# The opening of a one-layer encoder kernel: GpSimd's sums cut and held, square sums on ScalarE, PSUM banks laid out by name

## The chip, the cores and the metric

The kernel runs on one core of a Trainium2 chip. A core has TensorE (PE in the profile; its weight loads are PEld), VectorE (DVE), ScalarE (ACT), GpSimd (POOL) and SyncE (SP), which issues most transfers. The metric is the device time of one execution in microseconds; the median of several runs is compared.

## What is computed

One layer of a macaron encoder over 1024 frames of width 1024 in float32: half a SwiGLU feed-forward (inner width 2816), stick-breaking attention with 16 heads, and half a second SwiGLU feed-forward, each behind an RMS norm.

```python
def rms_norm(x, gain):
    xf = x.astype(jnp.float32)
    y = xf * lax.rsqrt(jnp.mean(xf * xf, axis=-1, keepdims=True) + NORM_EPS)
    return (y * gain.astype(jnp.float32)).astype(x.dtype)

def swiglu(xn, w_in, w_out):
    gate, up = jnp.split(xn @ w_in, 2, axis=-1)
    return (jax.nn.silu(gate) * up) @ w_out
...
        x = x + 0.5 * swiglu(rms_norm(x, n1), wi1, wo1)
        x = x + stick_breaking_attention(rms_norm(x, mix_norm), *mix_params)
        x = x + 0.5 * swiglu(rms_norm(x, n2), wi2, wo2)
```

(The last three lines stand in a loop of one layer.) The change touches the norm in front of the first feed-forward, the first feed-forward itself, and the step from its first half to its second.

## The kernel before

**Numbers.** Every float32 operand of a product is split into two parts of the type that TensorE multiplies: `hi`, a rounded copy, and `lo`, the difference. A product is then three matmuls (hi hi, hi lo, lo hi; lines 308 to 310 in `mm3`, line 324 in `mm3_late`, which puts the third of each behind by four so that a late `lo` doesn't stop it). The copy is mostly ScalarE's, the difference GpSimd's or VectorE's (`split`, lines 196 and 197).

**Opening (lines 669 to 849).** The 1024 rows of x lie in eight blocks of 128, loaded in the order 4, 5, 6, 7, 0, 1, 2, 3. For each block: the sum of squares in two halves (`square`: ScalarE's or VectorE's, with an accumulator), the mean of the halves (`rate`, line 707, on GpSimd) and its power of -1/2 (line 711, GpSimd), the scaling of the rows (`scale`, line 714, VectorE), 128x128 transposes on TensorE into the banks `kb` (`turn_x`, line 743), and out of the banks `xh` on ScalarE (`high_x`, line 751) and `xl` on VectorE (`low_x`, line 754). Meanwhile the weights of the first pair of column blocks are split (`high`, `low`). The products of `first_pair` (line 849) follow in four steps: three units on rows 4 and 5 (256 columns), three units on rows 6 and 7, the fourth unit on all four, and all four units on rows 0 to 3. The callbacks `second_half` and `first_rows` put the transposes of the next rows ahead of the second, third and fourth step. Before the first transposes TensorE multiplies zeros (`IDLE`, line 687).

Rows 0 to 3 and 4 to 7 are also combined for the method of the later rounds, which needs seven products of half-size blocks in place of eight. `whole_x` (line 766, GpSimd) forms xh + xl of rows 4 to 7 in two halves of the width (`d` = 0 into `tl[0]`, `d` = 1 into `tl[3]`); `first_rows` subtracts these and others (lines 754 and 846).

**Order.** `go` chains the opening's instructions on each engine by hand: each may be issued only after the one that `go` put there last (`tc.issue_after`, an edge of order on one engine, not a wait between engines). The rest is ordered by the framework from priorities and its own estimate of times. `marks["open"]` puts the weight work of round 1 behind the opening.

**Rounds (`ffn_in`).** Ten rounds q = 1 to 10 follow; each makes the gate and the up projection of two column blocks by `seven`: products into banks `ka`, `kc` and two of `kb`, a copy out of a bank by ScalarE (line 498), a sum out of a bank by VectorE (line 502). `prepare` makes the seven weight operands, with sums on VectorE (line 475) and `unit`s, among them `s3`. Silu is ScalarE's (line 545), the product with the gate GpSimd's (line 552).

**Banks.** PSUM has eight banks of 128x512. `bank` takes a tile by name from the pool of the stage; a name gets its place when it is first asked for. In the opening that order is kc0, kb0, kb1, kb2, kb3, ka0, ka1, kc1. The next stage (`ffn_out`) lays out its own names ahead by `lay_banks`: ma0, ma1, mb0, mb1, ma2, ma3, mb2, mb3. Its first products go into ma0 to ma3 in turn; a bank may be written once the old one at its place has been read.

Of the kernel before, what the change touches and what calls it, by code (L numbers as in the profile page):

```python
# [67 lines left out]

IDLE = 13

# [43 lines left out]
def macaron_kernel(ctx, tc, x, g1, w1_in, w1_out, gm, w_qkv, gq, gk, w_o, g2, w2_in, w2_out, out):  # L114
# [51 lines left out]

    def lay_banks():

        p, _ = psum[-1]
        for tag, i in (("ma", 0), ("ma", 1), ("mb", 0), ("mb", 1), ("ma", 2), ("ma", 3), ("mb", 2), ("mb", 3)):  # L170
            p.tile([P, NHALF], F32, name=f"{tag}{i}", bufs=1)

# [123 lines left out]
    def go(engine, emit):  # L296

        with following(marks.get(engine)):
            marks[engine] = emit().ins
# [130 lines left out]
    def ffn_in(pl, w_in, keep, tl, hb, right, last):  # L430
# [35 lines left out]
        def prepare(raw, behind=None):  # L466
# [59 lines left out]
        for q in range(1, NQ):  # L526
# [17 lines left out]
            for g in gs.values():  # L544
                act.activation(g, g, AF.Silu)

# [117 lines left out]
    with pools(*RAWS) as pr:  # L664
# [3 lines left out]
        with banks("ps1"), pools(*STREAM) as pa:  # L668
            with pools("x") as px, pools("xs", side="right") as pl:
# [34 lines left out]
                def rate(tb, n=1):  # L704
                    to = slice(tb, tb + n)
                    for i in range(tb, tb + n):
                        go("pool", lambda: pool_e.tensor_scalar(
                            mean[:, i : i + 1], ss[:, 2 * i : 2 * i + 1], ss[:, 2 * i + 1 : 2 * i + 2], EPS,
                            op0=ALU.add, op1=ALU.add,
                        ))  # L710
                    go("pool", lambda: pool_e.tensor_tensor(r[:, to], mean[:, to], power.to_broadcast([P, n]), op=ALU.pow))

                def scale(tb, h):
                    go("dve", lambda: dve.tensor_scalar(
                        xs[tb][:, HALVES[h]], rows_of[tb][:, HALVES[h]], r[:, tb : tb + 1], None, op0=ALU.mult
                    ))

# [11 lines left out]
                def low(j, part, d, engine="pool", behind=None):  # L729
                    (hi, lo), src = us[j, part][d], src_of[j, part, d]  # L730
                    if behind is not None:
                        go("pool", lambda: pool_e.tensor_tensor(lo[:, 0, 0:1], behind, behind, op=ALU.mult))
                    e = pool_e if engine == "pool" else dve
                    go(engine, lambda: e.tensor_tensor(lo, src, hi.bitcast(F32), op=ALU.subtract))
# [27 lines left out]

                def whole_x(tbs):
                    c, q = slice(tbs[0] * P, (tbs[-1] + 1) * P), slice(tbs[0] % 4 * P, (tbs[-1] % 4 + 1) * P)
                    for d, t in ((0, tl[0]), (1, tl[3])):
                        go("pool", lambda: pool_e.tensor_tensor(
                            t[:, :, q], xh[:, 4 * d : 4 * d + 4, c].bitcast(F32),
                            xl[:, 4 * d : 4 * d + 4, c].bitcast(F32), op=ALU.add,
                        ))
# [14 lines left out]
                behind = xs[5][:, D - 1 :]  # L784
                for d in range(2):
                    high(0, 0, d)
                high(1, 0, 0, "dve")
                tps = turn_x((4, 5), range(KD))
                for d in range(2):
                    low(0, 0, d, behind=None if d else behind)  # L790
                high_x(tps, (4, 5))
                low_x(tps, (4, 5))
                high(1, 0, 1)
                for d in range(2):
                    low(1, 0, d)
                for tb in (6, 7):
# [9 lines left out]
                behind = xs[7][:, D - 1 :]  # L806
                for d in range(2):
                    high(1, 1, d)
                for d in range(2):
                    low(1, 1, d, behind=None if d else behind)  # L810
# [542 lines left out]
```

## Time and profile before

| | |
|---|---|
| median of 3 runs | 1954.4 us (1949.22 to 1956.27) |
| profiled execution, its own time | 1954.04 us |
| its span | 1952.3 us |
| mean granted clock of TensorE | 0.995 |
| busy share: TensorE, VectorE, ScalarE, GpSimd | 98%, 64%, 50%, 58% |
| moved by DMA | 259.70 MB, 133 GB/s mean |

The span goes from the first to the last instruction of the program. A row of the timeline has the start in us from the span's start, the busy time, the engine, the line of the kernel, the operation, out<-in by the kernel's names without buffer numbers, the shapes, the count of instructions that it merges, and in brackets the idle time of the engine before it and what ended it. A row by tile has the count and the shortest, median and longest duration in ns. A row by stretches has the stretch, its length, the busy time with the count of PE, PEld, DVE, ACT and POOL, the granted clock (1.00 is full speed), the DMA share and GB/s. The chain of work is followed back from the last instruction: at each step to what released it. A wait for several semaphores is put down to the one that came last.

### The profile page before, as it was taken

The numbers are of one execution on the slowest core, as the hardware profiler recorded it, in microseconds if no ns is written. First come the engines' busy times: TensorE is split into PE (matmuls) and PEld (weight loads), VectorE is DVE, ScalarE is ACT, GpSimd is POOL, SyncE is SP. The second block draws the span as 40 slices with busy tenths as digits, with TensorE's granted clock in tenths as the row PEclk, the third lists the DMA queues.
The fourth block names the chain that finished last, engine by engine and source line by source line (L and its number), as shares of the span: only waits on it lengthen the run. The fifth ranks groups of instructions, "written<-read, shape, count | busy, mean of one in ns | idle before, by whom it ended". The sixth has DMA issues, their size and how long they took to land.

```text
span 1952.3 us, 26654 instructions
## 1 busy us (share of the span) xinstructions
PE 1910.8 (98%) x9357; PEld 1626.4 (83%) x9357; DVE 1249.9 (64%) x1727; ACT 977.8 (50%) x1787; POOL 1122.7 (58%) x997
## 2 busy tenths in 40 slices
PE   7999999999999999999999999999999999999999
PEld 7778888887888899898889887788888888888887
DVE  7855555545665757878877788467645645547645
ACT  5433333343334457777777787344433443343332
POOL 6766666765545746556556564214666666755554
PEclk8999999999999999999999999999999999999999
DMA  5233332337997410111011135421323332369973
GB/s 200 68 100 119 103 103 87 124 106 254 324 329 256 166 34 28 38 44 55 28 39 44 50 116 170 158 78 54 129 92 113 109 103 87 124 205 345 330 269 144
DMA packets 169560, 259.70 MB, mean 133 GB/s; under 512 B 11729, under 2 KB 82385, under 8 KB 169425
## 3 DMA queue, kind: packets, MB, share of 16 engines
q1 hardware_dynamic: 169280, 258.00, 38.9%
q8 instruction: 73, 1.20, 0.3%
q14 instruction: 63, 0.51, 0.1%
q10 hardware_dynamic: 144, 0.00, 0.0%
HBM read 197.66 MB, written 60.29 MB: 132 GB/s over the span
## 4 chain that ended last, share of the span: by engine, by line
PE 84%; DVE 7%; POOL 3%; ACT 3%; issue 2%; DMA 1%; DVEq 0%; SPq 0%; ACTq 0%; POOLq 0%
PE ka L308 6%; PE ka L309 6%; PE ka L310 6%; PE kc L310 4%; PE kc L308 4%; PE kc L309 4%; PE ma L308 4%; PE ma L309 4%; PE ma L310 4%; PE bq L308 4%; PE bq L309 4%; PE bq L310 4%; PE kb L310 3%; PE kb L308 3%; PE kb L309 3%; PE bo L1099 3%
## 5 line engine op out<-in xcount | busy, mean ns | idle before, releaser
L197 POOL TENSOR_TENSOR rp<-raw,rp 128x1024 fp32r<-128x1024 f32 x84 | 210.8, 2514 | 175.4 <-ACT rp L196 156.0
L197 POOL TENSOR_TENSOR u<-sf,u 128x512 fp32r<-128x512 f32 x160 | 227.7, 1426 | 133.2 <-ACT u L196 130.7
L197 POOL TENSOR_TENSOR u<-raw,u 128x512 fp32r<-128x512 f32 x128 | 183.8, 1438 | 159.5 <-ACT u L196 158.8
L1059 POOL TENSOR_TENSOR w<-w,om 128x512 f32<-128x512 f32 (+4 forms) x128 | 140.8, 1104 | 115.0 <-DVE om L1052 88.7
L196 ACT ACTIVATE u<-sf 128x512 fp32r<-128x512 f32 x160 | 100.5, 630 | 199.1 <-PE kb L309 86.3
L446 DVE TENSOR_TENSOR h<-h 128x512 f32<-128x512 f32 x110 | 135.4, 1234 | 85.5 <-POOL h L552 84.8
L196 ACT ACTIVATE rp<-rh 128x1024 fp32r<-128x1024 f32 (+1 forms) x78 | 76.5, 984 | 207.3 <-issue 67.3
L308 PE MATMUL bq<-wqh,xh 128*128 128x384 f32 x512 | 174.6, 341 | 0.0
L310 PE MATMUL bq<-wqh,xl 128*128 128x384 f32 x512 | 172.2, 336 | 0.0
L309 PE MATMUL bq<-wql,xh 128*128 128x384 f32 x512 | 172.1, 336 | 0.0
L574 DVE TENSOR_TENSOR raw<-raw 128x1024 f32<-128x1024 f32 (+1 forms) x60 | 87.4, 1459 | 113.2 <-DMA raw<-w_out 96.9
L196 ACT ACTIVATE u<-raw 128x512 fp32r<-128x512 f32 x128 | 80.3, 631 | 150.6 <-PE ka L309 100.8
L308 PE MATMUL ka<-xh,u 128*128 128x512 f32 x352 | 138.0, 392 | 3.5 <-ACT s L498 3.5
L308 PE MATMUL ma<-rp 128*128 128x512 f32 x352 | 137.8, 392 | 2.7 <-DVE h L502 2.7
L309 PE MATMUL ka<-xl,u 128*128 128x512 f32 x352 | 137.6, 391 | 0.0
L310 PE MATMUL ka<-xh,u 128*128 128x512 f32 x352 | 137.5, 391 | 0.0
L310 PE MATMUL ma<-rp 128*128 128x512 f32 x352 | 137.4, 390 | 0.0
L309 PE MATMUL ma<-rp 128*128 128x512 f32 x352 | 137.4, 390 | 0.0
L1050 ACT ACTIVATE w<-bz,f 128x512 f32<-128x512 f32 (+2 forms) x192 | 112.4, 585 | 44.6 <-PE bz L1046 39.4
L552 POOL TENSOR_TENSOR h<-h,g 128x512 f32<-128x512 f32 x80 | 112.9, 1411 | 36.1 <-DVE h L502 33.1
L475 DVE TENSOR_TENSOR sf<-raw 128x512 f32<-128x512 f32 x80 | 81.3, 1017 | 78.0 <-POOL u L197 78.0
L197 DVE TENSOR_TENSOR rp<-rh,rp 128x1024 fp32r<-128x1024 f32 (+1 forms) x70 | 113.2, 1635 | 22.1 <-ACT rp L196 19.6
(308 smaller groups left out, 5520.4 us busy)
## 6 DMA issues: line engine op xcount, KB each, us to landing
raw<-w_out SPq DMA_DIRECT2D x120, 512.0 KB, 5.6
raw<-w_in SPq DMA_DIRECT2D x86, 512.0 KB, 3.6
k<-h SPq DMA_DIRECT2D x154, 256.0 KB, 2.1
rh<-k SPq DMA_DIRECT2D x64, 512.0 KB, 6.2
raw_qkv<-w_qkv SPq DMA_DIRECT2D x64, 192.0 KB, 3.0
x_keep<-x SPq DMA_DIRECT2D x32, 256.0 KB, 3.5
x<-x_keep SPq DMA_DIRECT2D x32, 256.0 KB, 5.2
raw<-w_out SPq DMA_DIRECT2D x24, 256.0 KB, 4.2
```

The lines of the kernel that those rows point to most:

```text
L196: first = act.activation(hi, raw, AF.Copy).ins
L197: return first, (engine or dve).tensor_tensor(lo, raw, hi.bitcast(F32), op=ALU.subtract).ins
L308: pe.matmul(dst, ah, bh, start=start and i == 0, stop=False, skip_group_check=onto)
L309: pe.matmul(dst, ah, bl, start=False, stop=False, skip_group_check=onto)
L310: pe.matmul(dst, al, bh, start=False, stop=stop and i == n - 1, skip_group_check=onto)
L446: dve.tensor_tensor(src, hb[of[0]], hb[of[1]], op=getattr(ALU, of[2]))
L475: dve.tensor_tensor(f[n], x, y, op=op)
L552: pool_e.tensor_tensor(h, h, gs[k], op=ALU.mult)
L574: dve.tensor_tensor(w[0], w[0], w[1], op=getattr(ALU, W_OF[m][2]))
L1050: act.activation(to, z, AF.Sigmoid, scale=state["f", half][:, sign, tb % 4, hd : hd + 1])
L1059: pool_e.tensor_tensor(wt[:, c1 : c0 + n], wt[:, c1 : c0 + n], om[:, c1 - 1 : c0 + n - 1], op=ALU.mult)
L1099: pe.matmul(ot[:, :n], vv, t[:, c : c + n], start=start, stop=stop)
```

## The change

- 18 products of zeros ahead of the first transposes instead of 13.
- The opening lays out its banks by name: kc0, ka0, ka1, kb0, kb1, kb2, kb3, kc1.
- The means go from GpSimd (one small operation for each block) to VectorE (one for each call of `rate`); the power stays on GpSimd.
- All square sums of rows 0 to 3 are ScalarE's (three halves were VectorE's).
- Row block 4 is scaled by ScalarE; the copy of one first weight half goes from ScalarE to VectorE.
- `whole_x` takes one half of the width at a time, in two pieces of 128x512 instead of one of 128x1024. Only rows 4 and 5, half 0, stay ahead of the scalings of rows 0 to 3. The rest follows them: the first of these is held by a one-column GpSimd operation that reads row block 3's scaled rows.
- Rows 0 and 1 are scaled before the means of rows 2 and 3 are formed.
- In round 2 the four Silus may be issued on ScalarE only after the copy for `s3`, as `prepare` has last made it.

```diff
-IDLE = 13
+IDLE = 18
...
-    def lay_banks():
+    def lay_banks(names=("ma0", "ma1", "mb0", "mb1", "ma2", "ma3", "mb2", "mb3")):
...
-        split(src, hi, lo, engine)
+        marks["unit"], _ = split(src, hi, lo, engine)
...
             us["s3"] = unit(pl, f["s3"], pool_e)
+            marks["s3"] = marks["unit"]
...
-                act.activation(g, g, AF.Silu)
+                with following(marks["s3"] if q == 2 else None):
+                    act.activation(g, g, AF.Silu)
...
+                lay_banks(("kc0", "ka0", "ka1", "kb0", "kb1", "kb2", "kb3", "kc1"))
                 idle = bank("kc")
...
-                    for i in range(tb, tb + n):
-                        go("pool", lambda: pool_e.tensor_scalar(
-                            mean[:, i : i + 1], ss[:, 2 * i : 2 * i + 1], ss[:, 2 * i + 1 : 2 * i + 2], EPS,
-                            op0=ALU.add, op1=ALU.add,
-                        ))
+                    parts = ss[:, 2 * tb : 2 * (tb + n)].rearrange("p (t h) -> p t h", h=2)
+                    go("dve", lambda: dve.scalar_tensor_tensor(
+                        out=mean[:, to], in0=parts[:, :, 0], scalar=EPS, in1=parts[:, :, 1], op0=ALU.add, op1=ALU.add,
+                    ))
...
+                    if engine == "act":
+                        go("act", lambda: act.activation(to, x_, AF.Copy, scale=by))
+                    else:
+                        go("dve", lambda: dve.tensor_scalar(to, x_, by, None, op0=ALU.mult))
+
+                def hold(to, tb):
+                    last = xs[tb][:, D - 1 :]
+                    go("pool", lambda: pool_e.tensor_tensor(to, last, last, op=ALU.mult))
...
-                def whole_x(tbs):
+                def whole_x(tbs, d, behind=None):
...
+                    if behind is not None:
+                        hold(t[:, 0, q.start : q.start + 1], behind)
+                    for k in (0, 2):
+                        ks = slice(4 * d + k, 4 * d + k + 2)
                         go("pool", lambda: pool_e.tensor_tensor(
-                            t[:, :, q], xh[:, 4 * d : 4 * d + 4, c].bitcast(F32),
-                            xl[:, 4 * d : 4 * d + 4, c].bitcast(F32), op=ALU.add,
+                            t[:, k : k + 2, q], xh[:, ks, c].bitcast(F32), xl[:, ks, c].bitcast(F32), op=ALU.add
                         ))
...
-                for tb in (4, 5):
+                for tb, engine in ((4, "act"), (5, "dve")):
                     for h in range(2):
-                        scale(tb, h)
+                        scale(tb, h, engine)
...
-                square(0, 0)
-                square(0, 1)
-                square(1, 0)
-                square(1, 1, "dve")
+                for tb in range(2):
+                    for h in range(2):
+                        square(tb, h)
                 rate(0, 2)
-                whole_x((4, 5))
+                whole_x((4, 5), 0)
...
                     for tb in (2, 3):
-                        square(tb, 0)
-                        square(tb, 1, "dve")
-                    rate(2, 2)
-                    whole_x((6, 7))
-                    for tb in range(4):
+                        for h in range(2):
+                            square(tb, h)
+                    for tb in (0, 1):
                         for h in range(2):
                             scale(tb, h)
+                    rate(2, 2)
+                    for tb in (2, 3):
+                        for h in range(2):
+                            scale(tb, h)
+                    whole_x((6, 7), 0, behind=3)
+                    whole_x((4, 5), 1)
+                    whole_x((6, 7), 1)
```

More of the change, by code (lines that the diff above doesn't have):

```diff
@@ L165, in bank @@
         return p.tile([P, NHALF], F32, name=f"{tag}{i}", bufs=1)
-    def lay_banks():
+    def lay_banks(names=("ma0", "ma1", "mb0", "mb1", "ma2", "ma3", "mb2", "mb3")):
         p, _ = psum[-1]
-        for tag, i in (("ma", 0), ("ma", 1), ("mb", 0), ("mb", 1), ("ma", 2), ("ma", 3), ("mb", 2), ("mb", 3)):
-            p.tile([P, NHALF], F32, name=f"{tag}{i}", bufs=1)
+        for name in names:
+            p.tile([P, NHALF], F32, name=name, bufs=1)
     def any_bank(tags=ROUND):
@@ L705, in rate, with scale @@
                     to = slice(tb, tb + n)
-                    for i in range(tb, tb + n):
-                        go("pool", lambda: pool_e.tensor_scalar(
-                            mean[:, i : i + 1], ss[:, 2 * i : 2 * i + 1], ss[:, 2 * i + 1 : 2 * i + 2], EPS,
-                            op0=ALU.add, op1=ALU.add,
-                        ))
[L711 to L716, printed above, removed]
+                    parts = ss[:, 2 * tb : 2 * (tb + n)].rearrange("p (t h) -> p t h", h=2)
+                    go("dve", lambda: dve.scalar_tensor_tensor(
+                        out=mean[:, to], in0=parts[:, :, 0], scalar=EPS, in1=parts[:, :, 1], op0=ALU.add, op1=ALU.add,
+                    ))
+                    go("pool", lambda: pool_e.tensor_tensor(r[:, to], mean[:, to], power.to_broadcast([P, n]), op=ALU.pow))
+                def scale(tb, h, engine="dve"):
+                    to, x_, by = xs[tb][:, HALVES[h]], rows_of[tb][:, HALVES[h]], r[:, tb : tb + 1]
+                    if engine == "act":
[5 more added lines that the diff above has]
+                    go("pool", lambda: pool_e.tensor_tensor(to, last, last, op=ALU.mult))
                 us, src_of = {}, {}
@@ L731, in low @@
                     if behind is not None:
-                        go("pool", lambda: pool_e.tensor_tensor(lo[:, 0, 0:1], behind, behind, op=ALU.mult))
+                        hold(lo[:, 0, 0:1], behind)
                     e = pool_e if engine == "pool" else dve
@@ L761, in low_x @@
                         less(xl[:, k, c], tp, k, xh[:, k, c].bitcast(F32))
-                def whole_x(tbs):
+                def whole_x(tbs, d, behind=None):
                     c, q = slice(tbs[0] * P, (tbs[-1] + 1) * P), slice(tbs[0] % 4 * P, (tbs[-1] % 4 + 1) * P)
-                    for d, t in ((0, tl[0]), (1, tl[3])):
+                    t = tl[3 * d]
+                    if behind is not None:
+                        hold(t[:, 0, q.start : q.start + 1], behind)
+                    for k in (0, 2):
+                        ks = slice(4 * d + k, 4 * d + k + 2)
                         go("pool", lambda: pool_e.tensor_tensor(
-                            t[:, :, q], xh[:, 4 * d : 4 * d + 4, c].bitcast(F32),
-                            xl[:, 4 * d : 4 * d + 4, c].bitcast(F32), op=ALU.add,
+                            t[:, k : k + 2, q], xh[:, ks, c].bitcast(F32), xl[:, ks, c].bitcast(F32), op=ALU.add
                         ))
@@ L780, in macaron_kernel @@
                     rate(tb)
-                for tb in (4, 5):
+                for tb, engine in ((4, "act"), (5, "dve")):
                     for h in range(2):
-                        scale(tb, h)
-                behind = xs[5][:, D - 1 :]
-                for d in range(2):
-                    high(0, 0, d)
+                        scale(tb, h, engine)
+                high(0, 0, 0)
+                high(0, 0, 1, "dve")
                 high(1, 0, 0, "dve")
                 tps = turn_x((4, 5), range(KD))
-                for d in range(2):
-                    low(0, 0, d, behind=None if d else behind)
+                low(0, 0, 0, behind=5)
+                low(0, 0, 1)
                 high_x(tps, (4, 5))
@@ L793, in macaron_kernel @@
                 high(1, 0, 1)
-                for d in range(2):
-                    low(1, 0, d)
+                low(1, 0, 0)
+                low(1, 0, 1)
                 for tb in (6, 7):
@@ L805, in macaron_kernel @@
                         scale(6 + d, h)
-                behind = xs[7][:, D - 1 :]
                 for d in range(2):
                     high(1, 1, d)
-                for d in range(2):
-                    low(1, 1, d, behind=None if d else behind)
-                square(0, 0)
-                square(0, 1)
-                square(1, 0)
-                square(1, 1, "dve")
+                    low(1, 1, d, behind=None if d else 7)
+                for tb in range(2):
+                    for h in range(2):
+                        square(tb, h)
                 rate(0, 2)
-                whole_x((4, 5))
+                whole_x((4, 5), 0)
                 def second_half():
```

## The prediction

> **What bounds the kernel now.** The page first: TensorE is busy for 98% of the span, so only time in which it stands still, or runs at a low granted clock, can be won.
>
> ```profile
> span 1952.3 us, 26654 instructions
> PE 1910.8 (98%) x9357; PEld 1626.4 (83%) x9357; DVE 1249.9 (64%) x1727; ACT 977.8 (50%) x1787; POOL 1122.7 (58%) x997
> ```
>
> Then the view of who waited for whom: the total wait in us, how often, the longest. Three of its rows are TensorE's over the whole span, the last is ScalarE's in the first 90 us.
>
> ```profile
> PE kb L743 <- DVE xs L714: 8.3, 4, 3.6
> PE ka L308 <- ACT s L498: 3.5, 3, 2.4
> PE ma L308 <- DVE h L502: 2.7, 1, 2.7
> ...
> ACT xh L751 <- PE kb L743: 17.3, 7, 9.9
> ```
>
> The first is the opening: the transposes (L743) wait for VectorE's scaled rows (L714). The second lies in the first feed-forward, the third where that stage hands its PSUM banks to the next. The fourth says that ScalarE has room in the opening. The view by stretches gives the granted clock, the figure behind the five busy times:
>
> ```profile
> 5.24:8.66 3.42, 1.64 (x7) 0.89 (x5) 2.06 (x7) 2.18 (x6) 2.09 (x4) 1.00 1.16 315
> 8.66:12.07 3.41, 3.26 (x16) 3.26 (x16) 2.27 (x7) 2.29 (x6) 2.76 (x3) 0.50 1.01 380
> 12.07:15.49 3.42, 3.42 (x30) 3.42 (x30) 3.42 (x8) 3.42 (x10) 2.60 (x3) 1.00 1.09 376
> ...
> 35.96:39.38 3.42, 0.11 (x1) 0.11 (x2) 3.42 (x3) 0.00 (x0) 2.97 (x2) 0.50 0.00 0
> 39.38:42.79 3.41, 3.41 (x15) 3.31 (x16) 0.83 (x2) 2.50 (x4) 0.00 (x0) 0.50 0.23 82
> ...
> 462.63:466.04 3.41, 3.11 (x7) 2.48 (x8) 2.24 (x4) 1.06 (x1) 2.19 (x1) 0.50 0.82 281
> ```
>
> The reader is to see that a stretch of 3.41 us in which TensorE worked 1.64 us or less is followed by one at half clock. So a stall costs its own length and then up to 1.7 us more. Last, the chain of work, with start and length of each piece, shows the opening's path:
>
> ```profile
> 6.93 0.67 POOL mean L707
> ...
> 7.67 0.57 POOL r L711
> ...
> 8.27 0.50 DVE xs L714
> ...
> 8.81 3.43 PE kb L743 x15
> 12.24 5.75 PE ka L324 x48
> ...
> 20.87 1.76 PE kb L743 x16
> ...
> 42.31 5.76 PE kc L324 x24
> ```
>
> **Why VectorE is late at 32 us.** The timeline of VectorE, and of GpSimd beside it (start, busy time, operation, count, idle time before it):
>
> ```profile
> 25.36 2.76 DVE L699 SCALAR_TENSOR_TENSOR xs<-x 128x512 f32<-128x512 f32 x1
> ...
> 30.87 1.70 DVE L714 TENSOR_SCALAR xs<-x,r 128x512 f32<-128x512 f32 x4
> 32.78 6.83 DVE L714 TENSOR_SCALAR xs<-x,r 128x512 f32<-128x512 f32 x4 [0.22 <-POOL r L711]
> ...
> 31.97 0.77 POOL L711 TENSOR_TENSOR r<-mean,power 128x2 f32<-128x2 f32 x1
> 32.72 4.82 POOL L766 TENSOR_TENSOR tl<-xh,xl 128x1024 f32<-128x1024 f32 x2
> ...
> 54.31 1.30 POOL L846 TENSOR_TENSOR tl<-tl,tl 128x512 f32<-128x512 f32 x1 [15.38 <-DVE tl L754]
> ```
>
> Four scalings take 1.70 us where GpSimd runs no sum (30.87) and 6.83 beside its two sums of 128x1024 (32.78). A square takes 2.76 beside such a sum; alone 0.69 (the median below). One engine holds the other off for a whole instruction.
>
> **The change, step by step.** It moves no transfer, and no queue of DMAs.
>
> *Start: means on VectorE, 18 zero products, row 4 scaled on ScalarE.* The mean for row 5, 0.67 us on the path, becomes one 128x1 operation of VectorE with two columns in, which the trace doesn't have. It costs nothing at least, and at most about the 0.67 that it replaces; the nearest row, of the same engine and width, has 0.15, which I take:
>
> ```profile
> 72.51 0.15 DVE L474 TENSOR_SCALAR sf<-h 128x1 f32<-128x1 f32 x1
> ...
> 10.62 3.40 DVE L754 SCALAR_TENSOR_TENSOR xl<-kb,g_sb,xh 128x256 fp32r<-128x256 f32 x8 [1.14 <-ACT xh L751]
> ...
> L695 ACT ACTIVATE xs<-x x6: 617/624/632, 6.1 to 18.1; 128x512 f32<-128x512 f32 x6
> ...
> L699 DVE SCALAR_TENSOR_TENSOR xs<-x x3: 683/693/1618, 6.1 to 15.5; 128x512 f32<-128x512 f32 x3
> ```
>
> So row 5 is scaled from about 7.75 and its transposes start near 8.3, not at 8.81. The five added zero products, at full clock and 0.23 us from start to start (from 458.71 and 459.85 below, five steps), run into the wait for row 5 and end near 7.7: they delay nothing. TensorE then works some 2.9 us of 5.24:8.66, and the half clock behind it should go. All 16 transposes then take 1.76 (20.87) in place of 3.43 for 15, and end near 10.1 instead of 12.24: 2.1 us at most. But VectorE's eight corrections (3.40 us, now from about 9.7) end at 13.1, and the first 24 products wait for them; they end near 13.6, against 12.24 + 5.75 / 2 = 15.12. I take **1.5**, between 0 (landing rows or GpSimd's differences set the pace instead) and 2.1. Row 4's two scalings (2 x 0.62) lie on ScalarE before the first bank is full, and one raw copy leaves it for VectorE in exchange.
>
> *Square sums of rows 0 to 3 on ScalarE.* Three halves move, 3 x 0.62 = 1.9 us, and VectorE loses its two slowed squares (5.6 us from 25.36 to the scalings at 30.87). ScalarE's room covers them: its reads of the banks start near 19.9 (20.87 less 1.5, and a bank filled), take about 3.4 like the corrections, then four squares 2.5: near 25.8. Without that cover rows 2 and 3 are late one for one. The mean of rows 0 and 1 now stands in VectorE's order ahead of the eight corrections and waits for ScalarE's squares; by its count of six operations of 0.62 behind row 7's these end near 19.4, before the corrections can start, so 0.
>
> *GpSimd's sums in pieces, held.* Only (4,5), half 0, stays ahead of the scalings: two pieces of 128x512, 1.30 each by the row at 54.31. VectorE ends the corrections that stood before 25.36 near 23.9, may wait for a piece until 24.9, scales rows 0 and 1 (1.70) to 26.6, forms two means, GpSimd takes the powers (0.77), at 27.6 to 28.1, and rows 2 and 3 are scaled by 29.8. TensorE asks for them at 31.95 - 1.5 = 30.45. The wait goes:
>
> ```profile
> 31.95 0.60 PE L743 MATMUL kb<-ident,xs 128*128 128x128 f32 x2
> 35.39 0.33 PE L743 MATMUL kb<-ident,xs 128*128 128x128 f32 x1 [2.83 <-DVE xs L714]
> 39.27 3.04 PE L743 MATMUL kb<-ident,xs 128*128 128x128 f32 x13 [3.56 <-DVE xs L714]
> ```
>
> Idle 2.83 + 3.56 = **6.4**. The 13 transposes need 13 x 0.11 = 1.4 instead of 3.04, and 0.5 us of products ran at half clock to 42.79: **1.85** together. The hold waits for the last scaling; behind it on GpSimd stand six pieces (7.8 us), from 30 to 38, in time that is idle today (15.38 before 54.31). VectorE reads PSUM then, and needs the first two pieces near 36; they end near 32.5. Behind them stands a weight difference whose product TensorE reaches only at about 60. Late next: the scalings again; the margin at 30.45 is 0.7 to 1.5 us, thin.
>
> *Banks by name.* Today the next stage's third bank is the one that the last product of the stage before fills:
>
> ```profile
> 458.71 0.39 PE L308 MATMUL ma<-rp 128*128 128x512 f32 x1
> ...
> 459.85 0.39 PE L310 MATMUL ma<-rp 128*128 128x512 f32 x1
> 462.93 0.79 PE L308 MATMUL ma<-rp 128*128 128x512 f32 x1 [2.69 <-DVE h L502]
> ...
> 462.19 0.68 DVE L502 TENSOR_TENSOR h<-kb,s 128x512 f32<-128x512 f32 x1
> 462.79 1.22 DVE L197 TENSOR_TENSOR rp<-raw,rp 128x1024 fp32r<-128x1024 f32 x1
> ```
>
> TensorE issues six products into two banks, then waits for L502 to read kb3. By first use the order is kc0, kb0 to kb3, ka0, ka1, kc1, and the next stage's first four are places 0, 1, 4, 5: place 4 is kb3. In the new order these are kc0, ka0, kb1, kb2, all read earlier. The 2.69 goes, and of the half-clock stretch 3.1 / 2 = 1.55: **4.2**. Late next is the third chunk's operand, ready at 464.0 (L197) and asked for at 458.71 + 48 x 0.23 = 469.7: nothing.
>
> *Silu after the copy of s3, second round.* The stall of 2.4 in that round:
>
> ```profile
> 125.64 0.63 ACT L545 ACTIVATE g<-g 128x512 f32<-128x512 f32 x1 [5.67 <-DVE g L502]
> ...
> 127.33 0.50 PE L308 MATMUL ka<-xh,u 128*128 128x512 f32 x1 [2.36 <-ACT s L498]
> ```
>
> ScalarE's read of the bank stands behind a Silu that waits for VectorE. The mark, though, is the s3 of the gate itself, copied before its products began; as the order stands I cost the edge at **0**. With another order it may gain 2.4 + 1.7 = 4.1, or lose as much if a late copy holds four Silus.
>
> Sum: 1.5 + 6.4 + 1.85 + 4.2 = 13.95. The profiled execution took 1954.04 (1.74 around its span), 0.4 below the median of 1954.4. 1954.04 - 13.95 = **1940**.
>
> [...] 15 transposes filled 8.66:12.07, and the next stretch was granted 1.00. [...]
>
> **Rivals.**
> - *The stall at 127 us goes too*: 1936. For: a Silu stands in the way there. Against: the mark is another copy. 0.15.
> - *Opening alone*; the bank handover meets another late operand: 1954.0 - 9.75 = 1944. For: the operands come from the same three busy engines. Against: 5.7 us of margin. 0.15.
> - *Half the opening*: rows 2 and 3 are 2 to 4 us late; with the half clock behind, 4 to 6 lost: 1944 to 1946, and 1950 if the banks fail too. For: the thin margin. 0.18.
> - *No change*: the engines behind TensorE give it back, 1952 to 1956. For: their chain runs without slack into the first products after the opening. Against: it starts earlier by as much. 0.05.
> - *Slower*: the held sums starve. One sum waited out 9.30 us of VectorE's back-to-back operations on SBUF:
>
> ```profile
> L846 POOL TENSOR_TENSOR tl<-tl,tl x4: 1276/1297/9299, 54.3 to 67.3; 128x512 f32<-128x512 f32 x4
> ```
>
> If that met two of the six, 2 x 8 = 16 and two half clocks make 19 lost: 1959. It decides from 14 us lost. Against: beside VectorE's PSUM reads a sum took its 1.30. 0.05. [...]
>
> **How the numbers follow.** The forecast as written has 0.42. A change within 0.5%, 9.8 us, can't be told from none, so faster means below 1944.6: 0.42 + 0.15 + half of 0.15 = 0.65; same 0.30 (the rest of that, the half opening, no change); slower 0.05. The range leaves a tenth at each end: 1934 (both stalls gone, 2 us better), 1952 above. The likeliest case's own range is 1937 to 1943.
>
> **What would show it.** Right: no wait of L743 for L714 after 20 us, clock 1.00 from 5 to 50 us, products behind the first rows' transposes from 32 to 33 instead of 42.31, no wait of ma for L502. Wrong: rows 2 and 3 scaled after 31 us, a new wait in the first seven products, or the handover at its old length.

## The result and the profile after

The changed kernel takes 1935.53 us (median of four runs, 1933.84 to 1936.71) against 1952.52 for the kernel before beside it (1949.22 to 1956.27): a ratio of 0.9912, 95% interval 0.989 to 0.9933, so 17.0 us less. The forecast was 1940.0. The profiled execution shows 20.2 less (a span of 1932.1 against 1952.3). Both numbers are explained below, and why they differ.

First the page and TensorE's rows in the view of who waited for whom (us in all, times, longest). The rows of kb and ma are gone, and that of ka is at 1.9 instead of 3.5.

```profile
span 1932.1 us, 26665 instructions
PE 1905.4 (99%) x9362; PEld 1622.9 (84%) x9362; DVE 1243.5 (64%) x1726; ACT 981.8 (51%) x1794; POOL 1115.5 (58%) x994
...
PE ka L308 <- ACT s L499: 1.9, 2, 1.5
```

Then the opening in the timeline of TensorE, VectorE and GpSimd. Transposes are now L751, scalings L720, means L710, corrections L762, sums L778, the hold L724.

```profile
30.45 1.91 PE L751 MATMUL kb<-ident,xs 128*128 128x128 f32 x16
32.12 0.71 PE L324 MATMUL kc<-xh,u 128*128 128x512 f32 x2
...
37.67 2.59 PE L751 MATMUL kb<-ident,xs 128*128 128x128 f32 x16
40.02 0.70 PE L324 MATMUL ka<-xh,u 128*128 128x512 f32 x2
...
23.85 1.82 DVE L720 TENSOR_SCALAR xs<-x,r 128x512 f32<-128x512 f32 x4
25.59 0.15 DVE L710 SCALAR_TENSOR_TENSOR mean<-ss 128x2 f32<-128x2 f32 x1
26.56 1.67 DVE L720 TENSOR_SCALAR xs<-x,r 128x512 f32<-128x512 f32 x4 [0.82 <-POOL r L713]
...
34.13 2.73 DVE L762 SCALAR_TENSOR_TENSOR xl<-kb,g_sb,xh 128x512 fp32r<-128x512 f32 x4 [2.71 <-ACT tl L849]
36.77 2.71 DVE L762 SCALAR_TENSOR_TENSOR tl<-kb,g_sb,tl 128x512 f32<-128x512 f32 x4
...
21.65 2.55 POOL L778 TENSOR_TENSOR tl<-xh,xl 128x512 f32<-128x512 f32 x2
28.32 0.20 POOL L724 TENSOR_TENSOR tl<-xs 128x1 f32<-128x1 f32 x1 [1.79 <-DVE xs L720]
28.59 7.52 POOL L778 TENSOR_TENSOR tl<-xh,xl 128x512 f32<-128x512 f32 x6
```

The scalings of rows 2 and 3 take 1.67 instead of 6.83 and end at 28.2; the 16 transposes run through from 30.45 in 1.91, and the products follow at 32.12 instead of 41.96. Six pieces of GpSimd's sums lie behind the hold.

The same program was profiled a second time, and so was the kernel before. The table has the start of some of TensorE's pieces in each, from the timelines.

| piece of TensorE | before | changed | | before, again | changed, again | |
|---|---|---|---|---|---|---|
| first product of the opening | 11.93 | 9.62 | -2.31 | 10.54 | 10.04 | -0.50 |
| transposes of rows 0 to 3 | 31.95 | 30.45 | -1.50 | 31.37 | 30.87 | -0.50 |
| products behind them | 41.96 | 32.12 | -9.84 | 41.83 | 32.54 | -9.29 |
| products behind the next 16 transposes | 49.57 | 40.02 | -9.55 | 50.36 | 40.44 | -9.92 |
| sixth product of the first seven | 86.60 | 76.08 | -10.52 | 87.40 | 76.51 | -10.89 |
| round 2, behind the stall that stood at 127 | 131.78 | 118.77 | -13.01 | 131.01 | 119.22 | -11.79 |
| end of the rounds (first ma) | 458.71 | 445.17 | -13.54 | 457.93 | 445.62 | -12.31 |
| behind the handover (first mb) | 493.05 | 475.09 | -17.96 | 490.84 | 475.54 | -15.30 |
| attention, the piece ahead of the wait at 926 | 924.33 | 907.05 | -17.28 | 922.28 | 906.87 | -15.41 |
| behind that wait (bz) | 926.33 | 907.88 | -18.45 | 924.68 | 909.31 | -15.37 |
| behind the wait at 994 (bz) | 994.08 | 973.85 | -20.23 | 992.76 | 975.57 | -17.19 |
| last stage | 1918.38 | 1897.88 | -20.50 | 1917.33 | 1899.77 | -17.56 |

The right-hand pair agrees with the medians. The left-hand pair has more besides: half clocks of the kernel before at 8.66, 128 and 462 us, which its second profile lacks, and a wait in attention that the first profile of the changed kernel happened to miss. The second profile of the kernel before has half clocks of its own: 10.24 us of them from 34.38, where the first has 6.83, and 3.41 from 925.26, behind the first wait in attention.

### The profile page after: what moved, and what is told of

The parts are those of the page before. It is cut to its first block, busy times and chain, and to the rows that moved or that the text cites. A ratio compares the mean times of both kernels' runs of the same rounds, so it can differ in the third digit from the quotient of the medians.

```text
span 1932.1 us, 26665 instructions
## 1 busy us (share of the span) xinstructions
PE 1905.4 (99%) x9362; PEld 1622.9 (84%) x9362; DVE 1243.5 (64%) x1726; ACT 981.8 (51%) x1794; POOL 1115.5 (58%) x994
## 4 chain that ended last, share of the span: by engine, by line
PE 84%; DVE 8%; ACT 3%; POOL 2%; issue 2%; DMA 1%; DVEq 0%; POOLq 0%; ACTq 0%
PE ka L308 6%; PE ka L309 6%; PE ka L310 6%; PE kc L309 4%; PE kc L308 4%; PE kc L310 4%; PE ma L310 4%; PE ma L308 4%; PE kb L309 4%; PE kb L308 4%; PE kb L310 4%; PE ma L309 4%; PE bq L308 4%; PE bq L309 4%; PE bq L310 4%; PE mb L310 3%
## 5 line engine op out<-in xcount | busy, mean ns | idle before, releaser
L576 DVE TENSOR_TENSOR raw<-raw 128x1024 f32<-128x1024 f32 (+1 forms) x60 | 95.4, 1594 | 106.3 <-DMA raw<-w_out 95.5
L197 DVE TENSOR_TENSOR rp<-rh,rp 128x1024 fp32r<-128x1024 f32 (+1 forms) x70 | 107.7, 1555 | 22.2 <-ACT rp L196 19.6
```

The costliest lines, as they stand in the source:

```text
L197: return first, (engine or dve).tensor_tensor(lo, raw, hi.bitcast(F32), op=ALU.subtract).ins
L576: dve.tensor_tensor(w[0], w[0], w[1], op=getattr(ALU, W_OF[m][2]))
```

## Experiments

Each kernel is told by its edit against the kernel before or the changed one. Ratios are to the kernel before, run beside it.

**1. The kernel before, unaltered.** Is the forecast's picture, and what attention gained, a matter of one execution?

> The kernel before, unchanged, profiled a second time. In the first profile the attention had two waits of bz, 1.31 us at 926 and 1.68 us at 994, where the changed kernel has 0.15 at the same places; together with small ones this is 3.2 of the 20.2 us by which the spans differ. Theory A (they belong to that one execution): this profile has them elsewhere or not at all, and its span is 1949 to 1950. Theory B (the change removes them, by way of the time at which the attention starts): both are here again at the same places, span 1952.

1952.99 us. Both waits in attention stand again (1.73 at 924.68, 1.23 at 992.76), so they are no accident of the first profile. The half clocks at 8.66, 128 and 462 are not there: they come and go with the execution (experiment 2 has one at 127.84, experiment 3 one at 8.66).

**2. Banks alone**, on the kernel before:

```diff
+                lay_banks(("kc0", "ka0", "ka1", "kb0", "kb1", "kb2", "kb3", "kc1"))
                 idle = bank("kc")
```

> The kernel before, with nothing but the opening's banks laid out by name. Theory (the third bank of the next stage lay on kb3, which is read last): the wait of ma for L502 goes, the opening and the stall at 127 us stay as they were, and from the handover on everything is 4.2 to 4.5 us earlier. Rival (another operand of the next stage is late by nearly as much): 1 to 2 us. Rival (places don't matter): 0.

1950.23 us (ten runs), 0.9983, 0.9973 to 0.9992. The wait of ma for L502 is gone. From the first ma to the first mb this wins 4.4 us against the first profile of before (2.7 of wait, the rest half clock) and 3.0 against the second; the medians differ by 3.6. The waits of the opening are as before. The changed kernel's timeline at the same place:

```profile
444.94 0.39 PE L310 MATMUL kb<-t3h,u 128*128 128x512 f32 x1
445.17 0.39 PE L308 MATMUL ma<-rp 128*128 128x512 f32 x1
...
446.53 0.39 PE L308 MATMUL ma<-rp 128*128 128x512 f32 x1
446.75 0.39 PE L309 MATMUL ma<-rp 128*128 128x512 f32 x1
```

The third bank's product at 446.53 follows 0.23 behind the one before; the old kernel waited there.

**3. The held sums alone**, on the kernel before: `whole_x` in pieces, the hold, rows 0 and 1 scaled ahead of `rate(2, 2)`; means on GpSimd, squares on VectorE, 13 zero products.

```diff
-                    rate(2, 2)
-                    whole_x((6, 7))
-                    for tb in range(4):
+                    for tb in (0, 1):
                         ...
+                    rate(2, 2)
+                    for tb in (2, 3):
                         ...
+                    whole_x((6, 7), 0, behind=3)
+                    whole_x((4, 5), 1)
+                    whole_x((6, 7), 1)
```

> The kernel before, with GpSimd's sums in pieces and six of the eight held behind the scalings, and rows 0 and 1 scaled ahead of the means of rows 2 and 3; means, squares, zero products and banks as before. Theory (GpSimd's sums hold VectorE off): the squares on VectorE take at most 1.9 us each, the scalings 0.45, rows 2 and 3 are scaled by about 32, TensorE waits less than 0.5 us there and the products after the first rows' transposes start near 34.2 instead of 42.0; the time falls by 7 to 8 us. Rival (the squares on VectorE are what makes the rows late): half of that, 3 to 4 us.

1942.76 us, 0.9948, 0.9933 to 0.9963. TensorE and VectorE in its timeline:

```profile
32.00 1.91 PE L743 MATMUL kb<-ident,xs 128*128 128x128 f32 x16
33.66 0.71 PE L324 MATMUL kc<-xh,u 128*128 128x512 f32 x2
...
28.67 1.70 DVE L714 TENSOR_SCALAR xs<-x,r 128x512 f32<-128x512 f32 x4
30.59 1.67 DVE L714 TENSOR_SCALAR xs<-x,r 128x512 f32<-128x512 f32 x4 [0.22 <-POOL r L711]
```

The scalings end at 32.26, and no transpose waits. This one part is worth 8.3 us at the products (41.96 to 33.66); the square sums, the rival, aren't needed for it. At the first ma it is 11.6 ahead (447.07 against 458.71), about the 11.1 by which the medians differ, so it carries most of the change. The profile is that of the slowest of four runs, 1946.40, and loses part of this again to half clocks at 452, 917 and 985 us.

**4. The changed kernel with the sums where they stood**, in pieces but not held:

```diff
                 rate(0, 2)
                 whole_x((4, 5), 0)
+                whole_x((4, 5), 1)
...
                     rate(2, 2)
+                    whole_x((6, 7), 0)
+                    whole_x((6, 7), 1)
...
-                    whole_x((6, 7), 0, behind=3)
-                    whole_x((4, 5), 1)
-                    whole_x((6, 7), 1)
```

> The changed kernel, with GpSimd's eight pieces put back ahead of the scalings: those of rows 4 and 5 before the scalings of rows 0 and 1, those of rows 6 and 7 before the scalings of rows 2 and 3, none held. Theory (GpSimd's sums hold VectorE off): a scaling beside a piece takes 1.3 to 1.8 us instead of 0.45, rows 2 and 3 are scaled 3 to 4 us later, TensorE waits 2 to 4 us at 30.5 and runs a stretch at half clock: 4 to 5 us slower than the changed kernel. Rival (the squares' move to ScalarE alone is what counts): no slower than the changed kernel.

1939.72 us, 0.993, 0.9911 to 0.9948; 4.2 more than the changed kernel. Its four runs spread from 1936.56 to 1943.96 and the two intervals overlap, so the cost is read from the trace, where the first ma stands at 450.86 against 445.17 and 445.62.

```profile
31.13 0.49 PE L751 MATMUL kb<-ident,xs 128*128 128x128 f32 x3
33.59 1.86 PE L751 MATMUL kb<-ident,xs 128*128 128x128 f32 x13 [1.97 <-DVE xs L720]
...
24.52 3.79 DVE L720 TENSOR_SCALAR xs<-x,r 128x512 f32<-128x512 f32 x4
29.21 5.74 DVE L720 TENSOR_SCALAR xs<-x,r 128x512 f32<-128x512 f32 x4 [0.82 <-POOL r L713]
```

Smaller pieces didn't protect VectorE: four scalings take 3.79 and 5.74 beside them, where four take 1.67 in the changed kernel, and the wait is back, with a half clock from 34.87 to 38.28. It is the pieces' place behind the scalings, which the hold keeps, that does it.

**5. The changed kernel with 13 zero products; 6. 18 zero products on the kernel before; 7. 8 zero products.** One line each (`IDLE = 13`, `18`, `8`). Five products more or less are ten instructions of TensorE, a product and its weight load each (9362 of each on the changed kernel's page, 9357 before), and the suspicion was that they matter in attention, 900 us later.

> The changed kernel with 13 zero products again. Theory (the five products count twice: in the opening they keep TensorE working through 5 to 8.7 us, and, as ten more instructions of TensorE, they move its 16 KB instruction fetches off two stores of the attention): in the opening 0 to 1 us, less if the clock's stretches fall otherwise in this execution; and the fetch stands again about 1 us behind the issue of two stores o_keeph, which land after some 4 us instead of 2, so that the two waits of bz for w come back: 1.2 to 1.8 us each. In all 3 to 4 us slower than the changed kernel. Rival (the two waits went because of the earlier time at which the attention starts, or of other instructions): 0 to 1 us slower, no such waits.

> The kernel before with 18 zero products and nothing else. Theory (fetches): the two waits of bz at 926 and 994 shrink or go, 1.2 to 3.2 us, and the second stretch of the opening runs at full clock, 0.5 to 1 us: 2 to 4 us faster than before. Rival (they hang on the start time of the attention): 0 to 1 us faster.

> The changed kernel with 8 zero products in place of 18. Theory (ten TensorE instructions per five products move the fetches by about 1.2 us against the stores): compared with 13 products, where they fell 1.16 and 0.97 behind the issue of the two stores, they fall 1.2 later, near 2.2, behind the landing of 2.0, so that the second wait of bz (near 975) is gone again, and the first under 0.5. In the opening 8 products leave TensorE under 1.7 us busy in the stretch ahead of the transposes, so up to 1.7 us of half clock: first products 0.4 to 2 later. Rival (more zero products keep the clock up, and the waits in attention follow from that): both waits stand, 1.0 to 1.9, as with 13.

With 13: 1937.67 us, 0.9916, 0.9901 to 0.9931; its four runs (1937.15 to 1938.65) lie above all eight of the changed kernel (1933.84 to 1936.71). The first product of the opening is at 10.04, as in the second profile of the changed kernel, so nothing is lost there; both waits in attention are back (1.70 and 1.06). With 18 on the kernel before: 1952.11 (ten runs), 0.9989, 0.998 to 0.9999; the second wait is gone, the first stays (1.84). With 8: 1940.18 in one run; the first wait is gone, the second stays, and a third appears at 1045. So the waits move between stores with the count, as the theory has it; its arithmetic (1.2 us later for five products less, so clear of both) fell. In the opening 8 are too few:

```profile
1.64 3.78 PE L691 MATMUL kc<-xl 128*128 128x512 f32 x8 [1.64 <-POOL xl L685]
7.68 0.47 PE L751 MATMUL kb<-ident,xs 128*128 128x128 f32 x1 [2.26 <-ACT xs L718]
8.46 3.46 PE L751 MATMUL kb<-ident,xs 128*128 128x128 f32 x15 [0.30 <-DVE xs L720]
```

TensorE stands 2.26, then transposes at about half the pace: 15 in 3.46, where 16 take 1.91 in experiment 12.

**8. The changed kernel again; 9. its square sums back on VectorE; 10. its means back on GpSimd.**

> The changed kernel once more, unaltered. Theory (whether an instruction fetch meets the first of the two attention stores is decided anew in each execution once 18 zero products are issued): the wait of bz at about 908 us may stand here, 1.0 to 1.8, though it was 0.15 in the first profile; the one near 974 stays at 0.15; median 1935.5. Rival (it belongs to the program): 0.15 at both places again, as in the first profile.

```diff
-                for tb in range(2):
-                    for h in range(2):
-                        square(tb, h)
+                square(0, 0)
+                square(0, 1)
+                square(1, 0)
+                square(1, 1, "dve")
...
-                        for h in range(2):
-                            square(tb, h)
+                        square(tb, 0)
+                        square(tb, 1, "dve")
```

> The changed kernel with three of the eight half squares of rows 0 to 3 on VectorE again. Theory (the held sums alone free VectorE): the squares take 0.7 us each, at most one of them beside a piece; rows 2 and 3 are scaled 1.4 to 2 us later, at 29.6 to 30.2, still before TensorE asks at 30.45: no slower, 0 to 0.5 us. Rival (the squares had to go too): rows late by 1 us or more, 1 to 3 us slower.

```diff
-                    parts = ss[:, 2 * tb : 2 * (tb + n)].rearrange("p (t h) -> p t h", h=2)
-                    go("dve", lambda: dve.scalar_tensor_tensor(...))
+                    for i in range(tb, tb + n):
+                        go("pool", lambda: pool_e.tensor_scalar(...))
```

> The changed kernel with the means on GpSimd again, one small operation of 0.67 for each block. Theory (the mean of row 5 lies on the path to the first transposes, the others are covered): the transposes start 0.4 to 0.6 later than 7.78, the first products 0.4 to 0.6 later than 9.62, and rows 2 and 3 are scaled 0.7 to 1.2 later, near 29.0 to 29.4, still ahead of 30.45; 0.5 in all, median 1936.0. Rival (VectorE's turn through the mean held up its own squares, so GpSimd's is as good): no shift at 9.62, median 1935.5.

Again: 1936.21 us, 0.992, 0.9899 to 0.994. The first wait in attention stands here (1.77 at 909.31), the second doesn't: whether the first store lands late differs between executions of one program (after 4.4 here, 2.5 in the first profile).

Squares back: 1935.62 us, 0.9904, 0.9888 to 0.9921, the time of the changed kernel. TensorE is 1.0 later than in the first profile of the changed kernel from 11 us on, for another cause than the squares: a weight copy on VectorE (L735) takes 1.51 us, and TensorE waits 0.72 behind it. This part is worth nothing measurable.

Means back: 1935.68 us, 0.9917, 0.99 to 0.9935, the same again. But its VectorE shows what the part buys:

```profile
24.55 3.46 DVE L721 TENSOR_SCALAR xs<-x,r 128x512 f32<-128x512 f32 x4
29.01 1.68 DVE L721 TENSOR_SCALAR xs<-x,r 128x512 f32<-128x512 f32 x4 [1.00 <-POOL r L714]
```

The means delay GpSimd's two pieces, which start at 24.20 instead of 21.65, so the first scalings run beside those and take 3.46; the means of rows 2 and 3 stand behind the pieces. The last scaling ends at 30.7, 0.4 ahead of TensorE's 31.13 there; in the changed kernel the margin is 30.45 - 28.2 = 2.2. The expectation (29.0 to 29.4) missed this; no wait arises all the same.

**11. Silus of round 2 behind the read of the bank that s2 comes from; 12. the same with the low part of the head output in its own tile.** In the changed kernel the stall in round 2 stands as before, only shorter. TensorE, then ScalarE:

```profile
115.92 0.50 PE L308 MATMUL ka<-xh,u 128*128 128x512 f32 x1 [1.45 <-ACT s L499]
...
114.23 0.63 ACT L547 ACTIVATE g<-g 128x512 f32<-128x512 f32 x1 [4.76 <-DVE g L503]
114.77 0.61 ACT L196 ACTIVATE u<-sf 128x512 fp32r<-128x512 f32 x1
115.28 0.58 ACT L499 ACTIVATE s<-ka 128x512 f32<-128x512 f32 x1
```

A Silu and a copy that follows it keep ScalarE from reading ka. The program is the same, instruction for instruction, with and without the change's own edge (on s3), so that edge does nothing. The read that matters is s2's:

```diff
-                act.activation(s, b, AF.Copy)
+                marks["read"] = act.activation(s, b, AF.Copy).ins
...
             s2 = copy(a)
+            marks["s2"] = marks["read"]
...
-                with following(marks["s3"] if q == 2 else None):
+                with following(marks["s2"] if q == 2 else None):
```

> The changed kernel, with the Silus of round 2 issued behind ScalarE's read of the bank of s2 instead of the copy of s3; on every other engine the order of instructions is the same. The edge on s3 itself leaves the order of all engines as it is without it. Theory (ScalarE's read of the bank stands behind a Silu that waits for VectorE): the wait of 1.45 us at 116 us goes, nothing new takes its place, 1.4 us faster than the changed kernel. Rival (VectorE's own work is late, and TensorE meets it one product later): less than 0.5 us, with a new wait for VectorE or GpSimd between 116 and 125 us.

1935.02 us, 0.9902, 0.9887 to 0.9917. ScalarE now reads the bank first:

```profile
112.36 0.58 ACT L499 ACTIVATE s<-ka 128x512 f32<-128x512 f32 x1
114.51 0.63 ACT L547 ACTIVATE g<-g 128x512 f32<-128x512 f32 x1 [1.56 <-DVE g L503]
```

The next products start at 114.57, 1.35 earlier than in the changed kernel, though its opening was 0.28 later: 1.6 won there, with no new wait of ka. That much is below what the medians can tell.

Number 12 adds, in `values`:

```diff
-                    oh, ol = (
-                        pl["w"].tile([P, T - i * P], F32R, name=f"w1{i}", bufs=1)[:, :NHALF] for i in (2, 3)
-                    )
+                    oh = pl["w"].tile([P, T - 3 * P], F32R, name="w13", bufs=1)[:, :NHALF]
+                    ol = o.bitcast(F32R)
```

> The changed kernel with the Silus of round 2 behind the read of s2's bank, and with the low part of the head output made in its own tile, so that the late store of the high part has only the tile that is needed last. Theory (the waits at 908 and 974 are a store that lands late ahead of the next use of its tile): no bz wait over 0.3 us at either place wherever the fetch falls; 0 to 2 us below the kernel with the Silus alone (1935.0): 1933 to 1935. Rival (the order of attention's instructions, which shifts with the changed tiles, counts for more than the two waits): over 1935, with new waits between 860 and 1450 us.

1934.00 us (1932.91 to 1934.56), 0.9907, 0.989 to 0.9924; the changed kernel beside it ran 1935.76 to 1936.65. By these four runs each it beats the changed kernel by about 2 us, and no other kernel here is below it. No wait of bz for w is over 0.3, although the store lands as late as ever; the rows are in the section on the hardware. But the rival's new waits came as well: TensorE waits 1.45 for GpSimd (bt, L1093) at 1192.49, and from the first bz to the last this profile needs 605.6 us, the second one of the changed kernel 605.9. So how much of the 2 us attention gave is open; 1.4 of it is there at the first ma (444.19 against 445.62), ahead of attention.

## Why the forecast was nearly right

*The opening, 9.75 forecast with its start: 9.84 and 9.29 measured at the products behind the first rows' transposes.* The long term holds. GpSimd's sums held VectorE off: in the kernel before the two scalings that begin at 32.78 and 35.26 end at 35.33 and 37.81, 0.28 behind the sums beside them (35.05 and 37.53). Out of its way they give back the wait and its half clock (experiments 3 and 4). The scalings ended at 28.2 where 29.8 was the limit given, so half the opening, the rival, did not come. Six pieces took 7.52 on GpSimd where 7.8 was forecast: none starved, which was the rival that ended slower. The square sums were costed at nothing, and experiment 9 shows no difference. Taken alone, from the transposes' start to the products, this part was 8.25 in the sum and is 8.34 in the first pair and 8.79 in the second, where the kernel before stood at half clock for longer. In the second pair that hides part of what the start fell short by.

*Of it the start, 1.5 forecast: 1.50 in the first pair, 0.50 in the second.* The mean's price held. From VectorE's square of row 5 to the scaling of row 5 the kernel before needs 8.27 - 6.05 = 2.22 and the changed kernel 7.47 - 5.84 = 1.63, so 0.6 where 0.5 was forecast. (With the means back on GpSimd it is 7.97 - 6.12 = 1.85: row 5's mean takes 0.30 there. In the kernel before, where VectorE scales row 4 beside it, it takes 0.66.) Two other things were off. First the half clock at 8.66, the larger part of the 1.5: whether the kernel before has it differs by execution. With 13 products the first product stood at 11.93 and 11.99 in two profiles, at 10.54 and 10.51 in two others; 18 on the same kernel left it at 10.50. Second the zero products. "They end near 7.7 and delay nothing" took all of them at full clock. In the changed kernel they start 0.43 us apart from 2.24 to 5.65 and 0.23 apart from 5.95 on (its record of the clock begins, at full, at 5.78), and how long they take differs by execution:

```profile
1.64 6.30 PE L691 MATMUL kc<-xl 128*128 128x512 f32 x18 [1.64 <-POOL xl L685]
7.78 2.08 PE L751 MATMUL kb<-ident,xs 128*128 128x128 f32 x16
```

That is the changed kernel; in experiment 12, with the same 18:

```profile
1.64 7.24 PE L691 MATMUL kc<-xl 128*128 128x512 f32 x18 [1.64 <-POOL xl L685]
8.72 1.91 PE L751 MATMUL kb<-ident,xs 128*128 128x128 f32 x16
...
6.81 1.32 ACT L718 ACTIVATE xs<-x,r 128x512 f32<-128x512 f32 x2
```

There row 4 is scaled at 8.13, and its transposes start at 8.72 behind the zeros: 0.6 lost to them. Without enough of them 2.0 are lost (8 products, the first product at 11.57 against 9.62).

*Not in the sum, and against it: 0.7 behind the next transposes.* They take 37.67 to 40.02, 2.35 instead of 1.67. VectorE begins its corrections (L762) at 34.13, 2.71 idle behind a read of ScalarE's (L849), and the banks come free as it goes. In the second pair (48.70 to 50.36, 1.66, in the kernel before) 10.61 falls to 9.92 as well. The chain behind TensorE, named as the "no change" rival, does cost something, but not more than this, and 1.0 comes back by 76 us, where shorter waits of ka stand.

*Banks, 4.2 forecast: 4.42 in the first pair, 2.99 in the second.* The wait is gone whole. The half clock behind it, 1.55 of the sum, exists only in some executions of the kernel before.

*The edge on Silu, 0 forecast: 0.* The mark was the wrong one, as written. The stall at 127 yet shrank from 2.36 to 1.45, and 0.9 were won there in both pairs; the half clock behind it makes 2.5 of it in the first pair alone. This is a part of the rival that gave 1936; that rival's reason, the edge, is refuted. The 0.9 belongs to the held sums: experiment 3, which has them and no edge, stalls 1.42 there, experiment 4, which has the edge and not the hold, 2.36. By which path is open.

*Not in the sum at all: 1.8 in the second pair, 3.0 in the first, in attention.* The waits of bz at 926 and 994 were in the profile before, in no stage that the change touches, and the forecast took no account of them. This is the term that was missing. Of the 1.8, the shorter second wait is 1.1 (0.15 instead of 1.23), and 0.7 goes with the half clock at 925.26. What the runs show of these waits is in the last section.

The sum for the second pair: 9.92 behind the opening's transposes, 0.97 by 76 us, 0.90 at round 2's stall, 0.52 by the end of the rounds, 2.99 at the handover, 0.07 to behind the first wait in attention, 1.82 to behind the second, 0.37 after it: 17.56, against 17.0 of the medians. The forecast's 13.95 lacked attention's 1.8 and the 2.4 between 40 and 458 us, and had the clock's part of two terms too high. What was too high (start and banks, 2.2 together) hides about half of what was left out, 4.2; that much of the closeness is luck, the mechanisms of the opening and the banks are not. That the opening alone would count, the second rival, falls with experiment 2.

Transposes and the clock: the prediction has a stretch of 15 transposes and full clock behind it. In the changed kernel the clock stayed full around both sets of transposes, from 7.78 and from 30.45. Its view by stretches, cut at even times (granted clock behind POOL):

```profile
5.20:8.60 3.40, 3.40 (x17) 2.63 (x16) 2.15 (x8) 2.51 (x7) 1.28 (x3) 1.00 1.18 315
8.60:12.00 3.40, 3.40 (x26) 3.01 (x25) 2.95 (x9) 3.40 (x10) 3.32 (x4) 1.00 1.01 382
...
28.80:32.20 3.40, 3.40 (x33) 3.40 (x31) 0.69 (x1) 1.11 (x2) 3.40 (x3) 1.00 0.05 10
32.20:35.60 3.40, 3.40 (x17) 2.83 (x16) 1.47 (x3) 3.40 (x7) 3.40 (x4) 1.00 0.21 77
```

That is a weak test, because transposes fill only about half of a stretch here, and other products the rest. More telling are stretches at half clock in which almost nothing but transposes ran: 3.26 us of them in the kernel before (8.66:12.07) and 3.19 in experiment 3 were followed by full clock, as 3.11 of other products were (462.63:466.04 in the kernel before). 2.75 of transposes in the kernel with 8 zero products (7.32:10.73) were not, and neither were 2.73 of zero products alone in experiment 12 (0.96:4.37). (The clock's record begins with its first rise; in these last two the slow pace ahead of it was read as half clock: 0.23 us for a transpose instead of the 0.11 at 20.87 in the kernel before, 0.43 for a zero product instead of 0.23.) These few stretches show no difference between transposes and other products.

## What to carry to other kernels

Four scalings that took 6.83 us instead of 1.70 were not slow but held off: where a short vector operation takes several times its usual length, look at what GpSimd runs at that moment, and try to move that whole, behind a held instruction (1.67 here), rather than cut it up (5.74 in experiment 4). Profile the unaltered kernel twice before pricing a stall: the waits in attention came back here (1.73 and 1.23), the half clocks at 8.66, 128 and 462 did not. And name a bank's or a tile's next user, not only its size, when it is given a place: the handover (2.69 us of wait) and attention's waits (1.77) were both the right data in the place that was needed next.

## What the runs showed of the hardware

The profile has a queue of DMAs that it marks as instruction, and its packets (the fetches of the expectations) are found beside the late stores of attention. The row of the changed kernel's page (packets, MB, share):

```profile
q8 instruction: 73, 1.20, 0.3%
```

That is 16.4 KB a packet. There is one packet for 256 of the 2 x 9362 products and weight loads, and from one packet to the next TensorE starts 255 of them (median; 205 to 303); that they are TensorE's instructions is the author's inference from these counts. One packet takes 0.88 to 1.78 us in the first profile of the kernel before (median 1.02) and 0.88 to 1.84 in that of the changed one (median 1.06).

In the kernel before two packets began 0.96 and 1.00 behind the issue of a store of 256 KB (920.71 and 988.11), and these two stores landed after 3.92 and 4.27; of the other twelve of that line ten landed after 1.99 to 2.04, and the last two after 2.62 and 6.06. The first of the two packets ended at 923.16, and the last 16 packets of its store and of the low part's, issued next, came one behind the other from 923.14 to 924.81. In the second profile of the changed kernel one packet lies between 897 and 912, and the store landed after 4.4. Transfers at 897 to 912 (KB, us to landing), then ScalarE and TensorE:

```profile
o_keeph<-w SPq DMA_DIRECT2D x1, 256.0 KB, 4.4
...
907.72 0.47 ACT L1062 ACTIVATE w<-bz,f 128x256 f32<-128x256 f32 x1 [2.44 <-DMA o_keeph<-w]
...
909.31 0.39 PE L1058 MATMUL bz<-kh_s,q_s 128*128 128x256 f32 x1 [1.77 <-DVE w L1064]
```

ScalarE's write of the tile w waited 2.44 for the store that reads it; TensorE's next product into bz waited 1.77, the last of it for VectorE (L1064). In the first profile the packet began 2.00 behind the issue, the store landed after 2.5, and TensorE waited 0.15:

```profile
o_keeph<-w SPq DMA_DIRECT2D x1, 256.0 KB, 2.5
...
906.07 0.48 ACT L1062 ACTIVATE w<-bz,f 128x256 f32<-128x256 f32 x1 [0.57 <-DMA o_keeph<-w]
...
907.88 0.39 PE L1058 MATMUL bz<-kh_s,q_s 128*128 128x256 f32 x1 [0.15 <-DVE w L1064]
```

Experiment 12 shows the chain from its other end: the store lands late as before, but from the tile that is needed last, and TensorE's wait at this place is gone.

```profile
o_keeph<-w SPq DMA_DIRECT2D x1, 256.0 KB, 4.2
...
906.56 0.38 PE L1058 MATMUL bz<-kh_s,q_s 128*128 128x256 f32 x1 [0.16 <-DVE w L1064]
```

So five more products at the start of the program went with 1 to 2 us in a stage 900 us and more later (1937.67 with 13 against 1935.53 and 1936.21 with 18, waits of 1.70 and 1.06 with 13). That they do it by moving the packets against the stores is the author's reading; no run moved a packet alone. In 17 of the 19 stores that landed late at these places, over all profiles, the packet began 0.96 to 1.17 us behind the issue; what ties it to the store is open. In the other two (experiments 3 and 4) it began 2.05 and 2.04 behind, hardly later than in the first profile above, and yet the store landed after 4.5 and 4.4. So the start of the packet alone does not tell which store lands late.

The clock's record changed at steps of 3.41 us. In the kernel before the half clocks lasted 3.41 (8.66, 128.12 and 462.63) and 6.83 (35.96), and the full clock between them 23.89, 85.33 and 331.09: 7, 25 and 97 times 3.41. Cut in this way from the first full clock (5.24), its stretches at full clock with 1.64, 0.34, 1.05 and 1.01 us of TensorE's work (5.24, 32.55, 124.71, 459.22) were followed by half clock, and the one at 991.70, with 1.74, was not; so the wait of 1.68 at 994 cost no half clock, and that of 2.36 at 127 did. In the changed kernel the shortest ahead of the program's end had 2.34 (647.49), and the clock stayed full. Over all profiles, 18 of the 19 stretches at full clock with 1.73 us or less were followed by half clock, and one with more was (1.80, with 8 zero products). Of the stretches at half clock, the shortest that was followed by full clock had 2.94 us of work, and the longest that was not 2.75. Open is what sets where the stretches lie: the first full clock stands at 5.24 in the kernel before and at 5.78 in the changed one, and single terms of this case moved by 0.6 to 1.6 us between two executions of one program.
